# Feed-forward output projection computed by seven block products in place of eight, in three parts, with operands prepared in the feed-forward loop

## The chip, the cores and the metric

The kernel runs on one core of a Trainium2 chip. The metric is device time in microseconds (us) of one execution. A core has TensorE for matmuls (PE; its weight loads are listed apart, as PEld), VectorE (DVE), ScalarE (ACT), GpSimd (POOL) and SyncE (SP), which here only issues DMAs. ScalarE issues DMAs too (ACTq). Each engine works through its own list of instructions in order; semaphores order the engines against one another.

## The reference

One layer over 1024 tokens of width 1024, all in float32. Cut to what matters here:

```
x  = x + merged @ w_out                       # merged: four gated mixers
h2 = rmsnorm(x, g_ffn)
f_gate, f_up = split(h2 @ w_ffn_in, 2)        # w_ffn_in: 1024 x 5632
x  = x + (silu(f_gate) * f_up) @ w_ffn_out    # w_ffn_out: 2816 x 1024
h3 = rmsnorm(x, g_ple)
x  = x + sigmoid(h3 @ w_ple_gate) * (p @ w_ple_proj)
return rmsnorm(x, g_final)
```

## The kernel before

Activations lie transposed: a tile is 128 channels by 1024 tokens (512 KB). Each float32 matmul is made of three passes over reduced-precision parts: `split` writes a rounded part `hi` (copy on ScalarE) and the rest `lo` (subtraction on VectorE), and the product is hi·hi + hi·lo + lo·hi. Every matmul here is 128 x 128 by 128 x 512.

**Seven products.** The gate matmuls and the feed-forward input (`pair`, L537) compute two output tiles at once. Channels and tokens are cut in two blocks each, so that a 2 x 2 block product is done with seven block products in place of eight, at the price of sums: four over the weights (the generator `sums` in `pair`: L548, L551, L555, L557, on GpSimd), four over the activations (`operands`, L517, made once and kept in `OPS[p][i]`), and a few at the outputs. `product(p)` splits a weight sum (L563) into one of four buffers, and for four input pairs i runs three matmuls each (L568): 12 matmuls. Products 0, 2 and 4 accumulate in the same PSUM bank, with a ScalarE copy in between (L576, L583, L588). A call of `pair` is 84 matmuls.

**Feed-forward loop** (L695 to L715). 11 iterations over two hidden tiles each; an iteration is one `pair` for the gate and one for the up part, then silu and multiply. The two result tiles are stored to device memory by four DMAs of 256 KB on ScalarE's queue (L714).

**Feed-forward output** (L724 to L767). The 22 hidden tiles are the inner dimension and the 8 tiles of `x2` the outputs. `CHUNKS` cuts the inner dimension in two (14 and 8 hidden tiles), and `grp` the outputs in two groups of four. For each hidden tile the loop loads it (`load_parts`, L167), splits it, loads and splits its weights, and runs 4 x 3 x 2 matmuls (L740) into eight PSUM banks; the last part (L749 to L760) goes output tile by output tile. That is 22 x 8 x 3 x 2 = 1056 matmuls. `n3.add` (L767) then makes the parts and squares for the next norm: per tile two ScalarE and two VectorE operations of 1024 columns (L191, L192, L196, L200).

**Buffers.** `T` has 38 buffers of one tile; the feed-forward loop keeps 28 of them for `OPS` and one for the norm factor, and each `pair` takes two (`n15`, `n23`). `M` has 8, which before the loop pass to `x2` (L721). `W` has three for raw weights.

**Order.** A scheduler orders each engine's instructions ahead of time from the program's order and its own estimates: a weight split of the next pair can stand ahead of an output operation of this one. It also hands out buffers, in the order of the program.

Of the kernel before, what the change touches and what calls it, by code (L numbers as in the profile page):

```python
# [13 lines left out]
P = 128  # L14
# [10 lines left out]
CHUNKS = ((0, 14), (14, 22))  # L25
# [13 lines left out]
def mixers_kernel(ctx, tc, xT, pT, vec, mask, sgu_ln, sgu_wT, sgu_b, w_in, w_tok, w_gate, w_br, w_out,  # L39
# [26 lines left out]
    def M(name, w=S, dt=F32):  # L66
        return mp.tile([P, w], dt, tag="m", name=name, padded_shape=[P, S], bufs=8)
# [4 lines left out]
    def WS(name):  # L72
        return wp.tile([P, 512], F32, tag="sw", name=name, bufs=2)
# [278 lines left out]
    def qk(ct):  # L352
# [3 lines left out]
        for nm, i in (("q", 6 + ct), ("k", 8 + ct)):  # L356
            ps = proj_tile(i)
            t = T(f"{nm}{ct}")
            if nm == "q":
                nc.vector.scalar_tensor_tensor(t, ps, -(64.0 ** -0.5), rs, ALU.mult, ALU.mult)  # L360
                for h in range(2):
                    a, b = slice(h * 64, h * 64 + 64), slice(64 - h * 64, 128 - h * 64)
                    d = M(f"qs{ct}{h}", S, F32R)
                    nc.scalar.copy(d[a, :], t[a, :])
                    nc.vector.tensor_sub(d[b, :], t[a, :], d[a, :].bitcast(F32))
                    qs.append(d)
            else:
                nc.vector.tensor_mul(t, ps, rs)
                kl = M(f"kl{ct}", S, F32R)
                for h in range(2):  # L370
                    a, b = slice(h * 64, h * 64 + 64), slice(64 - h * 64, 128 - h * 64)
                    d = M(f"kd{ct}{h}", S, F32R)
# [60 lines left out]
    sgc = M("sgc", 6 * P).rearrange("p (g c) -> p g c", c=P)  # L433
# [83 lines left out]
    def operands(name, i, xa, xb, have=()):  # L517

        a1, a2, b1, b2 = xa[:, :512], xa[:, 512:], xb[:, :512], xb[:, 512:]
        t12, t34 = M(f"{name}t12i{i}"), M(f"{name}t34i{i}")  # L520
        t1, t2, t3, t4 = t12[:, :512], t12[:, 512:], t34[:, :512], t34[:, 512:]
        if 0 not in have:
            operand(name, 0, i, a1)
        nc.vector.tensor_sub(t1, a2, a1)
        operand(name, 1, i, t1)
        nc.vector.tensor_sub(t2, b2, t1)
        operand(name, 2, i, t2)
        if 3 not in have:
            operand(name, 3, i, b1)
        nc.vector.tensor_sub(t3, b2, a2)  # L530
        operand(name, 4, i, t3)
        if 5 not in have:
            operand(name, 5, i, b2)
        nc.vector.tensor_sub(t4, b1, t2)
        operand(name, 6, i, t4)

    def pair(name, wa, wb):  # L537

        ra = W(f"{name}ra")
        nc.sync.dma_start(ra, wa)  # L540
        rb = W(f"{name}rb")
        nc.sync.dma_start(rb, wb)
        a1, a2, b1, b2 = ra[:, :512], ra[:, 512:], rb[:, :512], rb[:, 512:]

        def sums():
            yield a1
            s1 = WS(f"{name}s1")
            nc.gpsimd.tensor_add(s1, b1, b2)  # L548
            yield s1
            s2 = WS(f"{name}s2")  # L550
            nc.gpsimd.tensor_sub(s2, s1, a1)  # L551
            yield s2
            yield a2
            s3 = WS(f"{name}s3")
# [6 lines left out]
        def product(p, src, ps, first):  # L561
            hi, lo = WP(f"{name}p{p}")
            split(hi, lo, src)  # L563
            for i in range(4):
                x = OPS[p][i]
                wh, wl = hi[:, i * P:(i + 1) * P], lo[:, i * P:(i + 1) * P]
                for n, (w, c) in enumerate(((wh, 0), (wh, 512), (wl, 0))):
                    nc.tensor.matmul(ps, w, x[:, c:c + 512], start=(first and i == 0 and n == 0),  # L568
                                     stop=(i == 3 and n == 2), skip_group_check=not first)
# [28 lines left out]
    def gate_operands(i):  # L598
# [6 lines left out]
        operands("g", i, xl[2 * i], xl[2 * i + 1], (0, 3, 5))  # L605
# [59 lines left out]
    for m0 in (0, 1, 2, 3, 4, 5, 6):  # L665
# [23 lines left out]
        if len(xgs) % 2 == 0:  # L689
            i = len(xgs) // 2 - 1  # L690
            operands("f", i, xgs[-2], xgs[-1])


    fd = []
    for j in range(0, NJ, 2):  # L695
# [28 lines left out]
    for ci, (k0, k1) in enumerate(CHUNKS):  # L724
        fs = {}
        for grp in range(2):
            last = ci == 1 and grp == 1
            if not last:
                ps = [[A(f"fo{ci}{grp}{mm}{h}") for h in range(2)] for mm in range(4)]
                for k in range(k0, k1):  # L730
                    if grp == 0:
                        fs[k] = load_parts(f"f{k}", fd[k])
                    if k % 2 == 0:
                        raw = W(f"fow{grp}{k}")
                        nc.sync.dma_start(raw, w_fo[:, (grp * NJ + k) * 512:(grp * NJ + k + 2) * 512])
                        w = w_parts(f"fow{grp}{k}", raw, S)
                    for mm in range(4):
                        for i, (n, p) in enumerate(((0, 0), (0, 1), (1, 0))):
                            for h in range(2):
                                nc.tensor.matmul(ps[mm][h], w[k % 2 * 4 + mm][n], fs[k].part(p, h * 512, h * 512 + 512),  # L740
                                                 start=(k == k0 and i == 0), stop=(k == k1 - 1 and i == 2))
            if ci == 1 and not last:
                for k in range(2):
                    raw = W(f"pp{k}r")
                    nc.sync.dma_start(raw, pT[k * P:(k + 1) * P, :])
                    pp.append(parts(f"pp{k}", raw))
            for mm in range(4):
                m = 4 * grp + mm
                if last:  # L749
                    pm = [A(f"fo{ci}{grp}{mm}{h}") for h in range(2)]  # L750
                    w = []
                    n = (k1 - k0) * P
                    for c in range(0, n, S):
                        e = min(c + S, n)
                        raw = W(f"fol{m}{c}", e - c)
                        nc.sync.dma_start(raw, w_fo[:, (NJ + k0) * 512 + mm * n + c:(NJ + k0) * 512 + mm * n + e])
                        w += w_parts(f"fol{m}{c}", raw, e - c)
                    for k in range(k0, k1):
                        for h in range(2):
                            mm_k(pm[h], w[k - k0], fs[k], k == k0, k == k1 - 1, ((h * 512, h * 512 + 512),), h * 512)  # L760
                else:
                    pm = ps[mm]
                for h in range(2):
                    t = x2[m][:, h * 512:h * 512 + 512]
                    nc.vector.tensor_add(t, pm[h], t)  # L765
                if ci == 1:
                    n3.add(m, x2[m])  # L767
# [101 lines left out]
def _layout(i):  # L869
# [15 lines left out]
    def taps(w):  # L885
# [22 lines left out]
    wo = a["w_ffn_out"][0].reshape(NJ, P, 2, 4, P)  # L908
    k1 = CHUNKS[1][0]
    out["w_fo"] = np.concatenate([t.reshape(P, -1) for t in (  # L910
        wo[:, :, 0].transpose(1, 0, 2, 3), wo[:k1, :, 1].transpose(1, 0, 2, 3), wo[k1:, :, 1].transpose(1, 2, 0, 3))], 1)
# [20 lines left out]
```

## Time and profile before

| | us |
|---|---|
| median of 3 runs | 1612.82 (1610.34 to 1613.44) |
| time of the profiled execution | 1612.55 |
| its span in the trace | 1610.8 |
| TensorE busy | 1588.8 (99%) |
| VectorE busy | 1031.6 (64%) |
| ScalarE busy | 640.0 (40%) |
| GpSimd busy | 215.1 (13%) |

The span runs from the first to the last instruction; 1.75 us of the execution's time lie around it. Busy shares are means over stages with different limits, so the rows below are read stage by stage. TensorE counts as busy while a matmul is under way; a matmul of 512 columns is listed with 389 ns, and the next may start before it ends.

### The profile page before, as it was taken

How to read it: one execution, taken by the hardware profiler on the slowest of the kernel's cores; microseconds unless marked ns; L12 is line 12 of the kernel's file. 1: busy time of each engine (PE TensorE's matmuls, PEld its weight loads, DVE VectorE, ACT ScalarE, POOL GpSimd, SP SyncE). 2: the span in 40 equal slices, each digit the busy share in tenths (PEclk: the TensorE clock that was granted, in tenths of full speed). 3: DMA queues.
4: the chain of work that ended last, by engine and by line, in shares of the span. 5: the costliest groups of instructions: out<-in, count | busy, mean ns of one | idle time of the engine just before them, and what ended most of it. 6: DMA issues, size and time to landing. Idle time of an engine off the chain costs nothing.

```text
span 1610.8 us, 19722 instructions
## 1 busy us (share of the span) xinstructions
PE 1588.8 (99%) x7626; PEld 1309.6 (81%) x7626; DVE 1031.6 (64%) x1506; ACT 640.0 (40%) x1068; POOL 215.1 (13%) x158
## 2 busy tenths in 40 slices
PE   9999999999999999999999999999999999999997
PEld 7976788778888888888888888888888888888886
DVE  6988785755567667686776666666666431354456
ACT  6335554233434334354553333433334411133334
POOL 0000000112222222200122322223220000000000
PEclk9999999999999999999999999999999999999998
DMA  6110233121212212213442222222225531211214
GB/s 223 53 40 14 70 129 108 66 79 47 92 53 72 66 52 73 66 59 135 140 176 79 85 79 87 94 82 79 81 89 172 207 92 53 68 41 46 66 47 141
DMA packets 46718, 140.93 MB, mean 87 GB/s; under 512 B 5280, under 2 KB 8608, under 8 KB 46624
## 3 DMA queue, kind: packets, MB, share of 16 engines
q1 hardware_dynamic: 39024, 125.98, 23.8%
q10 hardware_dynamic: 7600, 13.69, 2.3%
q8 instruction: 60, 0.98, 0.3%
q14 instruction: 34, 0.28, 0.1%
HBM read 115.53 MB, written 24.12 MB: 87 GB/s over the span
## 4 chain that ended last, share of the span: by engine, by line
PE 88%; DVE 8%; DMA 1%; ACT 1%; issue 0%; ACTq 0%; SPq 0%; DVEq 0%
PE fo L740 12%; PE pj L151 10%; PE wo L151 5%; PE br L151 5%; PE pg L151 5%; PE fo L151 3%; PE po L413 1%; PE sc L394 1%; PE pq L151 1%; PE ptp L407 1%; PE sc L393 1%; PE sp L317 1%; PE sp L315 1%; PE fu20u L568 1%; PE gt63u L568 1%; PE gt43u L568 1%
## 5 line engine op out<-in xcount | busy, mean ns | idle before, releaser
L330 DVE SCALAR_TENSOR_TENSOR cacc<-cy,vs,cacc 128x1023 f32<-128x1023 f32 (+29 forms) x60 | 75.7, 1263 | 0.5
L408 ACT COPY pt<-ptp 128x512 f32<-128x512 f32 (+3 forms) x48 | 21.8, 481 | 35.5 <-PE ptp L407 35.5
L814 DVE TENSOR_TENSOR pt<-pg,n3r 128x768 f32<-128x768 f32 (+1 forms) x16 | 11.0, 689 | 29.7 <-PE pg L151 29.7
L398 DVE CUSTOM_DVE_ANT_0 pr<-sc,maskt 128x128 f32<-128x128 f32 (+7 forms) x32 | 24.1, 753 | 9.1 <-PE sc L394 8.8
L151 PE MATMUL pj<-n1p,w1h 128*128 128x512 f32 x96 | 27.7, 408 | 1.4 <-ACT n1p L191 1.4
L765 DVE TENSOR_TENSOR x<-fo,x 128x512 f32<-128x512 f32 x32 | 20.9, 687 | 12.5 <-PE fo L151 11.3
L400 ACT ACTIVATE pr<-pr,nm 128x128 f32<-128x128 f32 (+7 forms) x32 | 24.9, 779 | 5.5 <-DVE nm L398 5.3
L438 POOL TENSOR_SCALAR_AFFINE_SELECT sgc<-sgc 128x512 f32<-128x512 f32 x1 | 1.3, 1322 | 168.8 <-DMA sgc<-in_sgu_wT 168.8
L151 PEld LDWEIGHTS pj<-n1p,w1h 128*128 128x128 f32 x96 | 18.7, 196 | 6.2 <-ACT n1p L191 2.2
L413 PE MATMUL po<-pt,vt 128*64 128x128 f32 x288 | 22.7, 279 | 0.2
L407 PE MATMUL ptp<-ident,pr 128*128 128x128 f32 x144 | 22.2, 276 | 0.0
L413 PEld LDWEIGHTS po<-pt,vt 128*64 128x64 f32 x288 | 16.9, 136 | 5.8 <-issue 2.8
L394 PE MATMUL sc<-kl,qs 64*128 64x512 f32 (+3 forms) x48 | 21.0, 438 | 0.0
L815 ACT ACTIVATE pt<-pt 128x768 f32<-128x768 f32 (+1 forms) x16 | 10.1, 630 | 26.3 <-DVE pt L814 26.3
L682 DVE TENSOR_TENSOR xr<-wo,xr 128x512 f32<-128x512 f32 x16 | 11.0, 688 | 14.8 <-PE wo L151 14.7
L407 PEld LDWEIGHTS ptp<-ident,pr 128*128 128x128 f32 x144 | 16.6, 140 | 3.1 <-ACT rb L418 1.0
L393 PE MATMUL sc<-kd,qs 128*128 128x512 f32 (+3 forms) x48 | 18.7, 390 | 0.1
L548 POOL TENSOR_TENSOR gt00s<-gt00rb 128x512 f32<-128x512 f32 x1 | 1.3, 1292 | 131.1 <-DMA gt00rb<-in_w_gate 131.1
L683 ACT ACTIVATE x1g<-xr,vs 128x512 f32<-128x512 f32 x16 | 11.6, 724 | 18.0 <-DVE xr L682 18.0
L394 PEld LDWEIGHTS sc<-kl,qs 64*128 64x128 f32 x48 | 8.8, 183 | 10.0 <-issue 8.6
L822 ACT ACTIVATE pt<-x 128x768 f32<-128x768 f32 (+1 forms) x13 | 8.4, 647 | 19.0 <-DVE x L818 19.0
L151 PE MATMUL pj<-n1p,w1l 128*128 128x512 f32 x48 | 15.3, 398 | 0.0
(4222 smaller groups left out, 5306.7 us busy)
## 6 DMA issues: line engine op xcount, KB each, us to landing
fow<-in_w_fo SPq DMA_DIRECT2D x18, 512.0 KB, 3.8
xg<-in_xT SPq DMA_DIRECT2D x8, 512.0 KB, 4.2
xr<-in_xT SPq DMA_DIRECT2D x8, 512.0 KB, 5.1
x1d<-xr SPq DMA_DIRECT2D x8, 512.0 KB, 2.9
x<-x1d SPq DMA_DIRECT2D x8, 512.0 KB, 5.8
x<-in_xT SPq DMA_DIRECT2D x7, 512.0 KB, 7.5
vpr<-in_w_tok SPq DMA_DIRECT2D x4, 512.0 KB, 4.8
spr<-in_w_tok SPq DMA_DIRECT2D x4, 512.0 KB, 3.6
```

The lines of the kernel that those rows point to most:

```text
L151: nc.tensor.matmul(ps[:, c - off:e - off], w[n], act.part(p, c, e), start=(first and i == 0), stop=(last and i == 2))
L330: nc.vector.scalar_tensor_tensor(acc[:, d:], y[:, :S - d], wj, acc[:, d:], ALU.mult, ALU.add)
L393: nc.tensor.matmul(sc[:, c:c + n], q, kd[h][:, c:c + n], start=True, stop=False)
L394: nc.tensor.matmul(sc[:, c:c + n], q[a, :], kl[a, c:c + n], start=False, stop=True)
L398: nc.vector.tensor_tensor_reduce(out=pr[:, :L], in0=sc[:, :L], in1=maskt[:, S - L:], scale=1.0, scalar=NEG, op0=ALU.add, op1=ALU.min, accu ...
L400: nc.scalar.activation(pr[:, :L], pr[:, :L], AF.Exp, bias=nm, scale=-1.0, accum_out=ls)
L407: nc.tensor.transpose(pa[:, j * P:(j + 1) * P], pr[:, c + j * P:c + (j + 1) * P], ident)
L408: nc.scalar.copy(pt[:, c:c + n], pa[:, :n])
L413: nc.tensor.matmul(po[h * 64:h * 64 + 64, :P], vtok[j // 4][:, hc:hc + 64], pts[h][:, j * P:(j + 1) * P], start=(j == 0), stop=(j == b))
L568: nc.tensor.matmul(ps, w, x[:, c:c + 512], start=(first and i == 0 and n == 0), stop=(i == 3 and n == 2), skip_group_check=not first)
L740: nc.tensor.matmul(ps[mm][h], w[k % 2 * 4 + mm][n], fs[k].part(p, h * 512, h * 512 + 512), start=(k == k0 and i == 0), stop=(k == k1 - 1 a ...
L765: nc.vector.tensor_add(t, pm[h], t)
```

## The change

The feed-forward output now goes through `pair`. The 22 hidden tiles are 11 input pairs, and `CHUNKS` cuts these into parts of 4, 4 and 3. In each part `pair` is called for four pairs of output tiles; with n input pairs a call has 7 x n x 3 matmuls. Its blocks are added to `x2`.

The seven activation operands of a hidden pair are made in the feed-forward loop (`operands("h", ...)`: four subtractions, seven splits), in buffers of `M`, and each is stored to device memory as it is made: seven DMAs of 512 KB per iteration on ScalarE's queue, in place of four of 256 KB. Each part of the output first loads its 28, 28 or 21 operand tiles into `T`, by SP. The splits of the hidden tiles in the output stage go away. The four weight sums of every `pair`, in the gates and the feed-forward input too, move from GpSimd to VectorE.

```diff
-CHUNKS = ((0, 14), (14, 22))
+CHUNKS = ((0, 4), (4, 8), (8, 11))
...
-    def operand(name, p, i, src):
-
-        t = T(f"{name}o{p}i{i}", F32R)
+    def operand(name, p, i, src, alloc=T):
+
+        t = alloc(f"{name}o{p}i{i}", F32R)
         split(t[:, :512], t[:, 512:], src)
-        OPS[p][i] = t
+        return t
+
+    def operands(name, i, a1, a2, b1, b2, have=(), alloc=T):
+
         t12, t34 = M(f"{name}t12i{i}"), M(f"{name}t34i{i}")
         t1, t2, t3, t4 = t12[:, :512], t12[:, 512:], t34[:, :512], t34[:, 512:]
+        for p, (src, sub) in enumerate(((a1, None), (t1, (a2, a1)), (t2, (b2, t1)), (b1, None), (t3, (b2, a2)),
+                                        (b2, None), (t4, (b1, t2)))):
+            if sub:
+                nc.vector.tensor_sub(src, *sub)
+            if p not in have:
+                yield p, operand(name, p, i, src, alloc)
...
         def sums():
             yield a1
-            s1 = WS(f"{name}s1")
-            nc.gpsimd.tensor_add(s1, b1, b2)
+            s1 = WS(f"{name}s1", w)
+            nc.vector.tensor_add(s1, b1, b2)
             yield s1
-            s2 = WS(f"{name}s2")
-            nc.gpsimd.tensor_sub(s2, s1, a1)
+            s2 = WS(f"{name}s2", w)
+            nc.vector.tensor_sub(s2, s1, a1)
...
-            nc.gpsimd.tensor_sub(s3, a1, b1)
+            nc.vector.tensor_sub(s3, a1, b1)
             yield s3
-            nc.gpsimd.tensor_sub(s2, a2, s2)
+            nc.vector.tensor_sub(s2, a2, s2)
...
-        for k in range(2):
-            d = tc.dram_tile([P, S], F32, name=f"fd{j + k}")
-            for h in range(2):
-                nc.scalar.dma_start(d[:, h * 512:h * 512 + 512], both[0][k, h])
-            fd.append(d)
+        f = both[0]
+        for p, t in operands("h", j // 2, f[0, 0], f[0, 1], f[1, 0], f[1, 1], (), M):
+            d = tc.dram_tile([P, S], F32, name=f"fd{p}{j}")
+            nc.scalar.dma_start(d, t.bitcast(F32))
+            fd[p].append(d)
...
-    for ci, (k0, k1) in enumerate(CHUNKS):
...
+    for ci, (i0, i1) in enumerate(CHUNKS):
+        n = i1 - i0
+        for p in range(7):
+            for i in range(n):
+                OPS[p][i] = T(f"ho{p}i{i0 + i}", F32R)
+                nc.sync.dma_start(OPS[p][i].bitcast(F32), fd[p][i0 + i])
+        if ci == 2:
+            for k in range(2):
+                raw = W(f"pp{k}r")
+                nc.sync.dma_start(raw, pT[k * P:(k + 1) * P, :])
+                pp.append(parts(f"pp{k}", raw))
+        c0, c1 = i0 * 2 * P, i1 * 2 * P
+        for m in range(0, KD, 2):
+            for k, h, ps, t in pair(f"fo{ci}{m}", w_fo[m, :, c0:c1], w_fo[m + 1, :, c0:c1], n):
+                x = x2[m + k][:, h * 512:h * 512 + 512]
+                nc.vector.tensor_add(x, x, t)
+                nc.vector.tensor_add(x, ps, x)
+            if ci == 2:
+                n3.add(m, x2[m])
+                n3.add(m + 1, x2[m + 1])
```

## Rows read from the trace of the kernel before

**Rows 1.** Page: busy time by engine; chain that ended last, by engine.

```profile
PE 1588.8 (99%) x7626; PEld 1309.6 (81%) x7626; DVE 1031.6 (64%) x1506; ACT 640.0 (40%) x1068; POOL 215.1 (13%) x158
...
PE 88%; DVE 8%; DMA 1%; ACT 1%; issue 0%; ACTq 0%; SPq 0%; DVEq 0%
```

**Rows 2.** Windows, columns as headed: gates; one loop iteration; output stage.

```profile
core 0: us, PE busy (x) PEld busy (x) DVE busy (x) ACT busy (x) POOL busy (x), PEclk, DMA share, GB/s
...
500.00:600.00 100.00, 100.00 (x443) 82.77 (x442) 69.47 (x102) 39.30 (x67) 23.57 (x16) 1.00 0.20 64
...
1035.10:1073.60 38.50, 38.38 (x170) 31.46 (x169) 25.42 (x34) 14.89 (x27) 10.75 (x8) 1.00 0.24 82
...
1232.70:1472.30 239.60, 239.60 (x1059) 198.40 (x1058) 94.75 (x116) 63.03 (x80) 0.00 (x0) 1.00 0.30 97
```

**Rows 3.** Timeline of TensorE (start us, us): where loop, output stage and tail begin.

```profile
806.52 0.62 PE L568 MATMUL fg0u<-fo0i,fg0p0h 128*128 128x512 f32 x2
...
1232.93 0.62 PE L740 MATMUL fo<-f0h,fow000h 128*128 128x512 f32 x2
...
1472.29 0.51 PE L151 MATMUL pq<-pp0h,wpp000h 128*128 128x512 f32 x2
```

**Rows 4.** Timeline of VectorE, beside GpSimd's work, in a dependent pair, and alone.

```profile
1040.91 1.67 DVE L709 TENSOR_TENSOR fg10n<-fg10n,fu10n 128x512 f32<-128x512 f32 x1
...
1043.70 0.68 DVE L704 TENSOR_TENSOR fu10n<-fu10n,n2r 128x512 f32<-128x512 f32 x1
1044.42 0.69 DVE L709 TENSOR_TENSOR fg10n<-fg10n,fu10n 128x512 f32<-128x512 f32 x1
...
1228.60 0.69 DVE L703 TENSOR_TENSOR fu20n<-fu20u,fu20n 128x512 f32<-128x512 f32 x1
1229.21 0.68 DVE L111 TENSOR_TENSOR fow00512l<-fow,fow00512h 128x512 fp32r<-128x512 f32 x1
1229.81 0.69 DVE L704 TENSOR_TENSOR fu20n<-fu20n,n2r 128x512 f32<-128x512 f32 x1
```

**Rows 5.** Timeline of GpSimd around the same time.

```profile
1040.35 1.68 POOL L557 TENSOR_TENSOR fg12s<-fg12ra,fg12s 128x512 f32<-128x512 f32 x1 [2.55 <-DVE fg12p2l L111]
```

**Rows 6.** Timeline of ScalarE: a store's issue, and the copy behind it.

```profile
1045.14 0.33 ACTq L714 DMA_DIRECT2D fd<-fg10n  x1
1045.51 0.59 ACT L576 COPY fg12n<-fg12u 128x512 f32<-128x512 f32 x1 [1.71 <-DVE fg10n L709]
```

**Rows 7.** Waits of TensorE's weight loads in the loop (us, times, longest).

```profile
PEld fg12u L568 <- ACT fg12n L576: 0.5, 1, 0.5
```

**Rows 8.** Windows of 5 us in which the DMA engines were nearly always busy.

```profile
810.00:815.00 5.00, 4.84 (x22) 3.72 (x21) 5.00 (x9) 4.10 (x8) 0.91 (x1) 1.00 0.93 347
815.00:820.00 5.00, 5.00 (x32) 4.39 (x31) 1.45 (x3) 2.58 (x5) 2.60 (x2) 1.00 0.77 285
820.00:825.00 5.00, 5.00 (x24) 4.09 (x23) 3.75 (x7) 1.69 (x4) 0.00 (x0) 1.00 0.95 372
```

**Rows 9.** DMA issues: count, KB each, median us from issue to landing.

```profile
fow<-in_w_fo SPq DMA_DIRECT2D x18, 512.0 KB, 3.8
...
fd<-fg12n ACTq DMA_DIRECT2D x4, 256.0 KB, 2.0
...
fd<-fg20n ACTq DMA_DIRECT2D x4, 256.0 KB, 3.0
```

**Rows 10.** Timeline of VectorE behind the last output tile.

```profile
1474.40 1.28 DVE L192 SCALAR_TENSOR_TENSOR n3l<-x,vs,n3h 128x1024 fp32r<-128x1024 f32 x1 [0.62 <-ACT n3h L191]
1475.60 1.22 DVE L200 TENSOR_TENSOR n3sq<-n3sq,n3sq 128x1024 f32<-128x1024 f32 x1
1476.74 0.68 DVE L111 TENSOR_TENSOR wpg01512l<-wpg01r,wpg01512h 128x512 fp32r<-128x512 f32 x1
```

**Rows 11.** Windows in which the granted clock fell.

```profile
1475.00:1480.00 5.00, 4.33 (x26) 3.82 (x25) 2.72 (x5) 2.37 (x4) 0.00 (x0) 0.81 0.08 26
1480.00:1485.00 5.00, 5.00 (x17) 4.32 (x16) 2.94 (x5) 0.41 (x1) 0.00 (x0) 0.50 0.00 0
```

More of the change, by code (lines that the diff above doesn't have):

```diff
@@ L70, in W, with WS @@
         return wp.tile([P, w], F32, tag="wr", name=name, padded_shape=[P, S], bufs=3)
-    def WS(name):
-        return wp.tile([P, 512], F32, tag="sw", name=name, bufs=2)
+    def WS(name, w=512):
+        return wp.tile([P, w], F32, tag="sw", name=name, padded_shape=[P, 512], bufs=2)
     def WP(name):
@@ L521, in operands @@
         t1, t2, t3, t4 = t12[:, :512], t12[:, 512:], t34[:, :512], t34[:, 512:]
[L522 to L534, printed above, removed]
@@ L535, in operands, with keep_operands @@
-        operand(name, 6, i, t4)
-    def pair(name, wa, wb):
-        ra = W(f"{name}ra")
+        for p, (src, sub) in enumerate(((a1, None), (t1, (a2, a1)), (t2, (b2, t1)), (b1, None), (t3, (b2, a2)),
[4 more added lines that the diff above has]
+                yield p, operand(name, p, i, src, alloc)
+    def keep_operands(name, i, xa, xb, have=()):
+        for p, t in operands(name, i, xa[:, :512], xa[:, 512:], xb[:, :512], xb[:, 512:], have):
+            OPS[p][i] = t
@@ L562, in product @@
             hi, lo = WP(f"{name}p{p}")
-            split(hi, lo, src)
-            for i in range(4):
+            split(hi[:, :w], lo[:, :w], src)
+            for i in range(n):
                 x = OPS[p][i]
                 wh, wl = hi[:, i * P:(i + 1) * P], lo[:, i * P:(i + 1) * P]
-                for n, (w, c) in enumerate(((wh, 0), (wh, 512), (wl, 0))):
-                    nc.tensor.matmul(ps, w, x[:, c:c + 512], start=(first and i == 0 and n == 0),
-                                     stop=(i == 3 and n == 2), skip_group_check=not first)
+                for j, (ww, c) in enumerate(((wh, 0), (wh, 512), (wl, 0))):
+                    nc.tensor.matmul(ps, ww, x[:, c:c + 512], start=(first and i == 0 and j == 0),
+                                     stop=(i == n - 1 and j == 2), skip_group_check=not first)
         src = sums()
@@ L604, in gate_operands @@
         OPS[0][i], OPS[3][i], OPS[5][i] = acts[2 * i].tiles[0], acts[2 * i + 1].tiles[0], acts[2 * i + 1].tiles[1]
-        operands("g", i, xl[2 * i], xl[2 * i + 1], (0, 3, 5))
+        keep_operands("g", i, xl[2 * i], xl[2 * i + 1], (0, 3, 5))
     ya = []
@@ L690, in mixers_kernel @@
             i = len(xgs) // 2 - 1
-            operands("f", i, xgs[-2], xgs[-1])
-    fd = []
+            keep_operands("f", i, xgs[-2], xgs[-1])
+    fd = [[] for _ in range(7)]
     for j in range(0, NJ, 2):
@@ L723, in mixers_kernel @@
     pp = []
-    for ci, (k0, k1) in enumerate(CHUNKS):
[L725 to L767, printed above, removed]
@@ new lines, in mixers_kernel @@
+    for ci, (i0, i1) in enumerate(CHUNKS):
+        n = i1 - i0
+        for p in range(7):
+            for i in range(n):
+                OPS[p][i] = T(f"ho{p}i{i0 + i}", F32R)
[14 more added lines that the diff above has]
+                n3.add(m + 1, x2[m + 1])
@@ L907, in _layout @@
     out["w_fi"] = halves(tiles(a["w_ffn_in"][0]))
[L908 to L911, printed above, removed]
+    wo = tiles(a["w_ffn_out"][0])
+    out["w_fo"] = np.concatenate([halves(wo[:, :, i * 2 * P:j * 2 * P]) for i, j in CHUNKS], 2)
     out["w_pg"] = tiles(a["w_ple_gate"][0])
```

21 lines of the change are left out of this document (11 added, 10 removed).

## The prediction

> **What bounds the kernel now.** The page comes first: TensorE is busy 99% of the span, and the chain that ended last runs 88% through it [rows 1]. So it is asked next whether a stage runs at TensorE's own rate or waits. The timeline answers for the output stage: its first matmul starts at 1232.93, the tail's first at 1472.29 [rows 3]. That is 239.36 us for 1056 matmuls, or 0.2267 us each, although each is listed with 0.39 us. The stage waits for nothing, VectorE is busy 94.75 of 239.6 us and the DMA engines 30% [rows 2]. Here fewer matmuls are time won, at 0.2267 us each, as long as nothing else becomes late.
>
> The loop starts at 806.52 and ends at 1232.93 [rows 3]: 426.4 us for 22 x 84 = 1848 matmuls, 418.9 us at that rate. 7.5 us are waits. An iteration takes 38.5 us; its 168 matmuls need 38.1, and 0.5 us is one wait of the weight load of product 2 for the copy of product 0's result [rows 7]. ScalarE's timeline shows why: the copy stands behind the issue of a store, which waited 1.71 us for the multiply it stores [rows 6], and that multiply took 1.67 us because GpSimd's sum ran beside it [rows 4, 5]. VectorE is busy 25.42 us of the iteration [rows 2], idle 13.1.
>
> **The change part by part.**
>
> *Matmuls.* 1056 become 4 x 7 x 3 x 11 = 924. 132 x 0.2267 = **29.9 us less**.
>
> *Weight sums to VectorE.* GpSimd took 1.68 us for one beside a VectorE operation [rows 5]. VectorE takes 0.69 for 512 columns, and the next independent one starts after 0.61, a dependent one after 0.72 [rows 4]. In the gates and the loop a pair gains four operations.
>
> *Operands in the loop.* Four subtractions, seven `lo` and seven `hi` per iteration. VectorE goes from 34 operations [rows 2] to 34 + 8 + 11 = 53: 53 x 0.61 = 32.3 us, or 38.2 if each depended on the one before, against TensorE's 38.1. ScalarE goes from 14.89 us to 14.89 + 7 x 0.59 plus three more issues of 0.33 [rows 6], about 20: no bound. Cost on the path: nothing below, if VectorE stays under 38 us; weight splits run up to four products ahead (four buffers, 10.9 us), which covers a burst. If that cover goes, a late split stops TensorE. Seven stores in place of four, each waiting for a `lo`: behind such an issue on ScalarE stands the copy that product 2 waits for, so the wait of 0.5 us can stay, go (5.5 us won over 11 iterations) or grow. I take 0: the multiply is no longer stretched by GpSimd, but there are more issues to wait behind. Bounds -5.5 and, from the rival below, +31.
>
> *Loading the operands.* This is what can eat the gain. A part's 28 tiles are 14.7 MB, and 28 of the 38 `T` buffers are the ones the pair before still reads. A buffer comes free when its three matmuls are done, every 3 x 0.2267 = 0.68 us, and its successor is needed one pair (84 matmuls, 19.04 us) later, again every 0.68 us. The DMA engines are slower. Nearly saturated they moved 335 GB/s on the mean of three windows and 372 in the best [rows 8]: 1.56 and 1.41 us per tile. I take the middle, 1.48. Landing adds 3.8 - 1.4 = 2.4 us [rows 9].
>
> Into part 1: of 38 buffers 28 hold `OPS`, one the norm factor, four the results in flight, so five tiles are loaded early. 23 remain, from 18.4 us before the loop's end to 18.4 us after it, when the last one is needed: 36.8 us. In that time also come two weight tiles and the last iteration's seven stores: 32 tiles x 1.48 + 2.4 = 49.8, **13.0 us late**. Best rate 10.7, mean rate 15.5; if the stores took their turn behind the loads, 25 tiles, 2.6. I count the stores: the last iteration's stores of 256 KB already landed in 3.0 us in place of 2.0 when loads ran beside them [rows 9]. The Trainium skill (DMA: Bandwidth & Descriptors, on queues, rings and completion order) says that each DMA engine takes turns between the queues that have work, packet by packet; the slower stores agree, and by that rule the stores delay the loads, 13.0 rather than 2.6.
>
> Into part 2: six spare buffers, 22 tiles and four of weights in 36.8 us: 26 x 1.48 + 2.4 = 40.9, **4.1 us late** (2.3 to 6.2). Into part 3: 15 tiles and three of weights need 29.0 us, and the last is due 32 us after the first release: nothing.
>
> `x2` can only load once `M` is free of the last iteration's operands, some 5 us past the loop's end, behind the tiles above. Its first use is three products into the first pair; VectorE would wait there, and behind it the next pair's splits. The wait above gives TensorE the same delay, so I count 0 (bound: eight loads ahead of the last operands, below).
>
> *Part 3 and the tail.* A pair is 63 matmuls, 14.3 us. VectorE has 11 operations of 384 columns (0.46 each by columns), 8 of 512 and `n3.add` twice, 1.20 + 1.14 from start to start [rows 10]: 5.0 + 4.9 + 4.7 = 14.6, so 0.3 us over per pair, 1.2 in all. Before, only tile 7's norm work stood behind the last matmul; now tile 6 is complete 2 us before the end, and part of its 2.3 us stands ahead of tile 7's: some 1 us more. **2.2 us**, bounds 0 and 6.
>
> *Elsewhere.* The gates' two extra microseconds of VectorE per pair lie under TensorE, where VectorE was busy 69.47 of 100 us [rows 2]. More DMA traffic costs no matmul: at 372 GB/s TensorE was busy all 5 us, with 24 matmuls under way, as many as elsewhere [rows 8].
>
> Sum: -29.9 + 13.0 + 4.1 + 2.2 = -10.6. From the profiled execution's 1612.55 that gives 1602.0; the median of the three runs is 0.27 above that execution, which changes nothing that can be measured: this kernel's runs can tell a change of about 0.2%, 3.2 us.
>
> **The rivals.**
>
> *Loads hidden.* If the stores fall behind the loads, or more buffers are spare than I count, part 1 is at most 2.6 us late. Against it stand the count of buffers and the slowed stores. With 2.6 and 2.3 at the transitions, 2.2 in the tail and the 5.5 us of loop waits gone: 1612.55 - 29.9 + 7.1 - 5.5 = 1584.
>
> *VectorE becomes the bound of the loop (slower).* The 13.1 us in which it idles per iteration are waits for casts and matmuls [rows 2], and the operands add a chain (subtract, cast on ScalarE, subtract) with more of them. It needs 32.3 us; the change loses as a whole when an iteration passes 38.5 + 10.6/11 = 39.5, that is when more than 7.2 of the 13.1 us remain idle. With nine it is 41.3, 2.8 more, 31 in 11 iterations: 1633; with eight, 1622. For it: VectorE takes its list in order, and an output operation that waits for TensorE holds all behind it. Against: it has 19 more operations to put in those gaps, and lead of several products.
>
> *Transitions worse (slower or equal).* With `x2`'s eight tiles ahead of the last operands and the mean rate: 40 x 1.56 + 2.4 - 36.8 = 28.0, and 6.2 into part 2: -29.9 + 34.2 + 2.2, 1619.
>
> *The clock.* In the tail, where TensorE was busy only 4.33 of 5 us, the granted clock fell to 0.81 and then 0.50, that is 1.2 GHz, for 5 us [rows 11]. Waits of a microsecond between products at a transition may do the same; while loads set the pace half speed costs nothing, as a product then takes 5.4 us against 4 x 1.48 = 5.9 for its tiles, and when that is over 5 us at half speed lose 2.5 us at each of two transitions: 1607. The Trainium skill (TensorE: Matmul & The Clock Gate, on oscillation) describes a matmul kernel whose clock fell at every wait for a DMA; the loop's waits of 0.5 us did no such thing here, with the clock at 1.00 [rows 2].
>
> **How the numbers follow.** My forecast, with part of the gain lost at the transitions (1594 to 1609, the clock's case within it): 0.45. Loads hidden, below 1594: 0.17. Within 3.2 us of no change, where a worse transition or one more microsecond per iteration leads: 0.12. VectorE as bound: 0.16. Transitions worse: 0.10. Faster 0.62, same 0.12, slower 0.26. The range for 8 in 10 leaves out the end of each side: 1585 to 1625. The likeliest case alone: 1594 to 1609.
>
> **What would show it.** The output stage's 924 matmuls at 0.2267 us, 209.5 us without waits; TensorE's waits there named by DMA of `ho` tiles, some 13 us before the first pair ends and 4 at the second part, with the DMA engines above 300 GB/s; none at the third. In the loop 53 VectorE operations per iteration, none stretched past 0.75 us, and iterations of 38 to 39 us. An iteration of 40 us or more with TensorE waiting for `lo` parts would make the prediction wrong on the slow side; an output stage below 215 us, on the fast side.

## The result, and the profile after

The changed kernel takes 1692.93 us (median of 4 runs, 1688.58 to 1693.8), the kernel before beside it 1611.58: a ratio of 1.0502 [1.0475, 1.0529]. The forecast was 1602.0 with a range to 1625. The change costs 81 us where 10.6 were to be won; between the two profiled executions it is 80.5.

Page of the changed kernel, busy time by engine and the chain that ended last [rows 1]:

```profile
PE 1583.7 (94%) x7494; PEld 1298.3 (77%) x7494; DVE 1202.3 (71%) x1909; ACT 702.0 (42%) x1211; POOL 1.1 (0%) x6
...
PE 85%; DMA 6%; DVE 6%; ACT 2%; issue 1%; ACTq 0%; SPq 0%; DVEq 0%
```

The 132 matmuls are gone (7626 to 7494), but TensorE's share fell from 99% to 94% of a longer span. DMA is now 6% of the chain. The timeline of TensorE says in which stage [rows 3]:

```profile
806.00 0.62 PE L564 MATMUL fg0u<-fo0i,fg0p0h 128*128 128x512 f32 x2
...
1276.62 0.62 PE L564 MATMUL fo00u<-ho0i,fo00p0h 128*128 128x512 f32 x2
...
1556.19 0.50 PE L151 MATMUL pq<-pp0h,wpp000h 128*128 128x512 f32 x2
```

The loop takes 470.6 us (426.4 before), the output stage 279.6 (239.4 before), the tail 135.1 up to the span's end (138.5 before). So +44.2 and +40.2, and both have to be explained. Windows of the gates, one iteration, the output stage, the first pairs of parts 1 and 2, the gap ahead of part 3, and part 3's first pair [rows 2] (a pair is counted from its first matmul to the next pair's first; in names parts count from 0, so `fo12` is the pair of output tiles 2 and 3 in part 2):

```profile
core 0: us, PE busy (x) PEld busy (x) DVE busy (x) ACT busy (x) POOL busy (x), PEclk, DMA share, GB/s
500.00:600.00 100.00, 100.00 (x443) 82.84 (x442) 74.39 (x118) 39.84 (x68) 0.00 (x0) 1.00 0.21 64
1060.20:1103.10 42.90, 40.22 (x170) 32.48 (x169) 33.21 (x54) 18.54 (x33) 0.00 (x0) 0.96 0.38 135
1276.60:1556.20 279.60, 220.97 (x926) 178.56 (x925) 159.53 (x253) 89.73 (x153) 0.00 (x0) 0.88 0.53 198
1276.60:1332.00 55.40, 24.38 (x85) 18.21 (x84) 19.69 (x33) 9.68 (x17) 0.00 (x0) 0.66 0.85 327
1389.10:1421.60 32.50, 21.57 (x85) 16.72 (x85) 10.71 (x17) 6.29 (x11) 0.00 (x0) 0.84 0.82 325
1478.70:1495.50 16.80, 0.23 (x2) 0.05 (x1) 3.02 (x4) 0.51 (x1) 0.00 (x0) 0.57 0.94 372
1495.50:1512.60 17.10, 17.10 (x63) 13.90 (x64) 13.09 (x25) 7.05 (x14) 0.00 (x0) 0.83 0.16 47
```

In the gates nothing changed but the engine of the sums. In the iteration VectorE has 54 operations in 33.21 us, as forecast, and is idle for 9.7; yet the iteration takes 42.9 us. In the output stage 924 matmuls at 0.2267 us are 209.5 us, so 70 us are waits: 36.4 in the first pair of part 1 (55.4 for 19.0), 13.5 in that of part 2, 16.8 ahead of part 3, and 2.9 in part 3's first pair, in which TensorE is busy throughout but at a granted clock of 0.83 (17.2 for 14.3). That makes 69.6.

**The loop.** Waits of TensorE's weight loads [rows 7], then ScalarE's timeline [rows 6]:

```profile
PEld fg12u L564 <- ACT fg12p4h L110: 3.1, 1, 3.1
```

```profile
1066.42 0.62 ACT L110 CAST ho2i<-ht12i 128x512 fp32r<-128x512 f32 x1
...
1070.24 0.62 ACT L110 CAST ho6i<-ht34i 128x512 fp32r<-128x512 f32 x1
1072.21 0.33 ACTq L710 DMA_DIRECT2D fd<-ho4i  x1
1072.81 0.33 ACTq L710 DMA_DIRECT2D fd<-ho5i  x1
1073.41 1.11 ACTq L710 DMA_DIRECT2D fd<-ho6i  x1
1074.57 0.59 ACT L575 COPY fg12n<-fg12q 128x512 f32<-128x512 f32 x1 [3.71 <-PE fg12c L564]
1075.05 0.59 ACT L579 COPY fg12n<-fg12u 128x512 f32<-128x512 f32 x1
1075.55 0.63 ACT L702 ACTIVATE fg12n<-fg12n 128x512 f32<-128x512 f32 x1
1076.08 0.60 ACT L110 CAST fg12p4h<-fg12s 128x512 fp32r<-128x512 f32 x1
```

TensorE waits 3.1 us for the cast of product 4's weights. Its sum was ready at 1070.97 (VectorE L551, from 1070.28, 0.69 us). The cast ran at 1076.08, because ScalarE's list has ahead of it the issues of three stores, which wait for the `lo` parts, and then two copies and a silu. The copy's bracket names a matmul of product 3, but the copy starts 0.05 us after the last issue ended (1073.41 + 1.11). All ten iterations after the first show such a wait, of 3.1 to 4.0 us. ScalarE is busy 18.54 of 42.9 us: it is late, not full.

The wait is not the whole price. The granted clock is 0.92 to 0.96 in each of these ten iterations, and TensorE is busy 39.7 to 41.0 us in them. Where the same list ran at 1.00 (the run with the load order, last section) it was busy 38.62. Over ten iterations that is some 15 us, an estimate from these rows; the other 29 of the 44.2 us are the waits, less the old 0.5 us per iteration.

**Part 1.** Timeline of SyncE's queue:

```profile
1259.10 0.33 SPq L538 DMA_DIRECT2D fo00rb<-in_w_fo  x1
1259.52 1.92 SPq L725 DMA_DIRECT2D ho0i<-fd  x4
...
1265.27 5.44 SPq L725 DMA_DIRECT2D ho2i<-fd  x4
1272.96 0.32 SPq L725 DMA_DIRECT2D ho3i<-fd  x1
1283.43 14.98 SPq L717 DMA_DIRECT2D x<-x1d  x8
1298.46 1.37 SPq L725 DMA_DIRECT2D ho3i<-fd  x3
1299.93 2.31 SPq L725 DMA_DIRECT2D ho4i<-fd  x4
1302.98 4.15 SPq L725 DMA_DIRECT2D ho5i<-fd  x4
1308.10 4.15 SPq L725 DMA_DIRECT2D ho6i<-fd  x4
```

The first operand load comes right behind a weight load, 17.1 us before the loop's end; no spare buffer was filled ahead. The eight `x2` loads stand in the middle of the operands. They wait for buffers of `M` until 1283.43, so that SyncE issues nothing for 10 us, and then take 15 us themselves. Fifteen operand tiles stand behind them. TensorE waits 20.0 us for `ho3i` and 10.6 in product 6, which stands ahead of products 2, 5 and 4 in its list and whose tiles are loaded last.

**Part 2 and part 3.** SyncE's queue again, then the matmul that waits in part 2, and the cast that waits in part 3:

```profile
1371.62 0.33 SPq L538 DMA_DIRECT2D fo10rb<-in_w_fo  x1
1372.00 2.66 SPq L725 DMA_DIRECT2D ho0i<-fd  x4
...
1398.41 4.15 SPq L725 DMA_DIRECT2D ho6i<-fd  x4
...
1484.97 0.33 SPq L536 DMA_DIRECT2D fo20ra<-in_w_fo  x1
```

```profile
1408.72 1.19 PE L564 MATMUL fo10e<-ho6i,fo10p6h 128*128 128x512 f32 x2 [10.63 <-DMA ho6i<-fd]
```

```profile
1494.89 0.51 ACT L110 CAST fo20p0h<-fo20ra 128x384 fp32r<-128x384 f32 x1 [18.92 <-DMA fo20ra<-in_w_fo]
```

Part 2's loads begin at 1372.00, two microseconds into the pair before (its first matmul is at 1370.1), right behind a weight load that got its buffer at 1371.62. The six spare buffers were not filled ahead. From 1377 to 1410 the DMA engines are full:

```profile
1377.00:1410.00 33.00, 22.07 (x94) 17.39 (x93) 13.25 (x21) 6.91 (x12) 0.00 (x0) 0.89 1.02 408
```

Product 6 runs ahead of product 2 on TensorE, but its tiles are loaded last. Ahead of part 3 it is the weights that are late: their load stands behind 21 operand loads.

### The profile page after: what moved, and what is told of

Read it like the earlier page. It is cut to its first block, busy times and chain, and to the rows that moved or that the text cites. A ratio compares the mean times of both kernels' runs of the same rounds, so it can differ in the third digit from the quotient of the medians.

```text
span 1691.3 us, 19947 instructions
## 1 busy us (share of the span) xinstructions
PE 1583.7 (94%) x7494; PEld 1298.3 (77%) x7494; DVE 1202.3 (71%) x1909; ACT 702.0 (42%) x1211; POOL 1.1 (0%) x6
## 4 chain that ended last, share of the span: by engine, by line
PE 85%; DMA 6%; DVE 6%; ACT 2%; issue 1%; ACTq 0%; SPq 0%; DVEq 0%
PE pj L151 10%; PE wo L151 5%; PE br L151 5%; PE pg L151 5%; DMA ho4i<-fd 2%; PE po L413 1%; DMA ho6i<-fd 1%; PE sc L394 1%; PE pq L151 1%; PE ptp L407 1%; PE sc L393 1%; DMA fd<-ho6i 1%; PE fg8u L564 1%; DMA ho2i<-fd 1%; PE fg20u L564 1%
## 5 line engine op out<-in xcount | busy, mean ns | idle before, releaser
L564 PE MATMUL fo00c<-ho3i,fo00p3h 128*128 128x512 f32 x8 | 3.9, 589 | 19.7 <-DMA ho3i<-fd 19.7
L678 DVE TENSOR_TENSOR xr<-wo,xr 128x512 f32<-128x512 f32 x16 | 11.0, 688 | 15.6 <-PE wo L151 15.6
L787 ACT ACTIVATE pt<-pt 128x768 f32<-128x768 f32 (+1 forms) x16 | 10.1, 630 | 26.3 <-DVE pt L786 26.3
L564 PEld LDWEIGHTS fo00c<-ho3i,fo00p3h 128*128 128x128 f32 x8 | 1.9, 279 | 20.8 <-DMA ho3i<-fd 20.7
```

Of the source, the lines that this page charges most:

```text
L564: nc.tensor.matmul(ps, ww, x[:, c:c + 512], start=(first and i == 0 and j == 0), stop=(i == n - 1 and j == 2), skip_group_check=not first)
L678: nc.vector.tensor_add(t, ps, t)
```

## The experiments

Each kernel's ratio is to the kernel before on the same chip.

**The sums alone** (kernel before, the four weight sums on VectorE).

```diff
-            nc.gpsimd.tensor_add(s1, b1, b2)
+            nc.vector.tensor_add(s1, b1, b2)
...
```

> The kernel before, with only the four weight sums of every pair moved from GpSimd to VectorE. Theory A (the loop's 44 us come from the operands and stores that stand in ScalarE's list ahead of the next weight cast; the sums are harmless): the loop keeps 426 us or loses the 0.5 us wait per iteration, so 1606 to 1613 us, the same within 0.4%. Theory B (VectorE's list is what makes weights late; eight more operations per iteration lengthen it): the loop grows by 10 us or more, 1622 or above.

Measured: 1605.85 us, ratio 0.9971 [0.9958, 0.9985]. One iteration:

```profile
1037.40:1075.50 38.10, 38.10 (x169) 31.54 (x169) 26.63 (x43) 14.88 (x26) 0.00 (x0) 1.00 0.26 83
```

The wait of 0.5 us for the copy [rows 7] is gone, and an iteration takes its matmuls' 38.1 us: theory A. This part of the change is a small gain, and this kernel is the fastest complete one of the study.

**The changed kernel with the sums back on GpSimd** (the four lines reversed).

> The changed kernel with the four weight sums back on GpSimd, all else as changed. Theory A: product 4 of the gate pair still waits for its cast behind the operand casts and store issues, the loop stays above 455 us (changed: 470.6) and the time above 1675. Theory B: with eight operations fewer on VectorE the loop falls to 430 to 440 us and the time to 1655 to 1662.

Measured: 1679.18, ratio 1.042 [1.0391, 1.0448]; iterations of 40.5 to 43.3, loop 453.6, output stage 281.4. Theory A's 455 is missed by 1.4 us, theory B's 430 to 440 by 13.6. The loop is 17.0 us better, but not cured, and most of the 17 is not work taken off VectorE: nine of its eleven iterations ran at a granted clock of 1.00, against one in the changed kernel. In the iterations from 1000 us on TensorE now waits up to 2.8 us for the third copy in place of the cast:

```profile
PEld fg16u L564 <- ACT fg16n L579: 2.8, 1, 2.8
```

It is still something in ScalarE's list, though VectorE has less to do: the waits are 2.3 to 3.4 us in place of 3.1 to 4.0. That leaves ScalarE's own list as the suspect.

**Operand stores issued by SyncE.**

```diff
-            nc.scalar.dma_start(d, t.bitcast(F32))
+            nc.sync.dma_start(d, t.bitcast(F32))
```

> The changed kernel with the seven operand stores per iteration issued by SyncE in place of ScalarE. Theory A, part issues: six issues that wait for lo parts leave ScalarE's list, the cast for product 4 comes 2 to 3 us earlier, iterations fall from 43 to 39 to 41 us, the time to 1650 to 1672. If the casts alone make it late (or theory B holds), iterations stay at 42 us or more and the time above 1680.

Measured: 1648.36, ratio 1.0229; loop 422.0 us. One iteration:

```profile
1036.30:1074.40 38.10, 38.10 (x169) 31.52 (x168) 33.15 (x54) 18.88 (x33) 0.00 (x0) 1.00 0.42 152
```

VectorE's and ScalarE's work is the same as in the changed kernel's iteration (33.15 and 18.88 us), the bytes are the same, and the iteration is 38.1 with the clock at 1.00, better than the 39 to 41 expected: all of the loop's 44 us, waits and clock, came from the store issues in ScalarE's list. (With them gone the copies also stand earlier in that list; the two weren't told apart.) The output stage stays at 281.5 us, with 59.9 in part 1's first pair.

**No operand loads** (stores by SyncE; the output stage loads no operands and multiplies by those that the loop holds, so its output is another).

```diff
-        for p in range(7):
-            for i in range(n):
-                OPS[p][i] = T(f"ho{p}i{i0 + i}", F32R)
-                nc.sync.dma_start(OPS[p][i].bitcast(F32), fd[p][i0 + i])
```

> Stores on SyncE, and no operand is loaded in the output stage: its products read the operands that the feed-forward loop left in its buffers, so the output is another. What is left is the output stage's own matmuls, weights, sums and the norm. If all its waits come from the loads, the stage takes 210 to 216 us (924 matmuls at 0.2267 are 209.5) against 281.5 with loads, and the time is 1577 to 1584 us. If VectorE, the weights or x2 hold it up too, the stage takes 225 us or more.

Measured: 1587.5, ratio 0.985 [0.9821, 0.9878]. The output stage:

```profile
1228.60:1446.70 218.10, 212.39 (x926) 174.43 (x925) 159.89 (x253) 90.05 (x153) 0.00 (x0) 0.98 0.27 91
```

218.1 us, 2 more than the 210 to 216 expected; the time, 1587.5, misses its 1577 to 1584 too. 8 us are lost in the second pair, where TensorE waits 6.0 for a cast whose weights `fo02rb` stand in SyncE's list behind the eight `x2` loads. Against 281.5 with the loads, exchanging the operands costs 63 us, and but for those 8 the stage needs its matmuls' time.

**`x2` loaded pair by pair, behind part 1's operands** (stores by ScalarE, as in the change).

```diff
-    for m in range(KD):
-        x2.append(M(f"x2{m}"))
-        nc.sync.dma_start(x2[m], x1d[m])
...
+            if ci == 0:
+                for k in range(2):
+                    x2.append(M(f"x2{m + k}"))
+                    nc.sync.dma_start(x2[m + k], x1d[m + k])
```

> The changed kernel with each pair of x2 tiles loaded in front of the pair of the first part that needs it, behind that part's operand loads in the program. Theory C (SyncE's list: the eight x2 loads wait for buffers of M ahead of the last 15 operand tiles): the first pair of part 1 falls from 55.4 to 30 to 36 us, as in part 2 (32.5), and the time to 1668 to 1676. Rival D (the transition is bound by what the DMA engines move): the pair stays above 48 us, as the same bytes have to come.

Measured: 1679.23, ratio 1.042. The first pair takes 42.8 us in place of 55.4, between theory C's 36 and rival D's 48; the second takes 20.3, the others are unchanged (32.9 in part 2). So `x2` ahead of the operands cost 12.6, and 24 us remain in part 1. There the DMA engines were full from 1255 to 1304 (share 1.01, 392 GB/s), from the first operand load, which again stood behind a weight load, to the last tile. So D's cause has a part in these 24.

**Operand tiles loaded in the order in which TensorE uses them.**

```diff
-        for p in range(7):
+        for p in (0, 1, 3, 6, 2, 4, 5):
```

> The changed kernel with each part's operand tiles loaded in the order of products 0, 1, 3, 6, 2, 4, 5, in which TensorE's list of the changed kernel first touches them, in place of 0 to 6. Theory E (part 2's first pair takes 32.5 us because TensorE's list has a piece of product 6 in fourth place, and its tile lands last, with three products queued behind it): that pair falls to 20 to 24 us and part 1's by about 10; 1668 to 1682 us. Rival D (the loading itself sets the length): part 2's first pair stays above 29 us.

Measured: 1690.51, ratio 1.0489; part 2's first pair 31.9 us against 32.5, and part 1's 55.2 against 55.4. Theory E is missed, and the rival's condition (above 29 us) is met. ScalarE's timeline in that pair:

```profile
1408.47 0.62 ACT L110 CAST fo12p0h<-fo12ra 128x512 fp32r<-128x512 f32 x1 [14.77 <-DMA fo12ra<-in_w_fo]
1408.99 0.58 ACT L579 COPY fo10n<-fo10u 128x512 f32<-128x512 f32 x1
```

The wait for `ho6i` is gone, and TensorE waits 5.0 us at product 5 and then 4.8 for this copy. The copy stands behind the next pair's first weight cast, whose load stands behind the operand loads. One order was mended, and the next one took its place; whether the loading itself would have held the pair as long, this run does not say.

**Weights first** (stores by SyncE, `x2` pair by pair; `then` are the part's operand loads, given to its first pair and so behind its weights; `pp` is loaded behind part 3's first pair).

```diff
-    def pair(name, wa, wb, n=4):
+    def pair(name, wa, wb, n=4, then=None):
...
         nc.sync.dma_start(rb, wb)
+        if then:
+            then()
```

> Stores on SyncE, x2 loaded pair by pair, and in each part the weights of the first pair loaded ahead of the operand tiles; the two tiles of p behind the last part's first pair. Theory F (at part 3 TensorE waits 16 us for weights that stand behind 21 operand loads in SyncE's list): fo16 to fo20 falls from 34.6 to 19 to 22 us; part 1's first pair, now with stores and loads in one list, 38 to 50. Time 1612 to 1628, against 1648 with the stores on SyncE alone. If part 3's operands are as late as its weights, the wait stays above 10 us and the time above 1628.

Measured: 1634.14, ratio 1.0139; stage 267.6. The gap ahead of part 3 is gone (`fo16` to `fo20` 19.1 us in place of 34.6), but part 3's first pair now takes 21.9 and waits 5.6 for operands, and the time misses 1612 to 1628. Part 2's first pair is 32.6, not moved. Part 1's is 52.7: less than with the stores on SyncE alone (59.9), but 10 us more than with `x2` pair by pair and the stores on ScalarE (42.8).

**A small first part** (as weights first, but stores by GpSimd; four parts, of at most 21 tiles, so that more `T` buffers are spare).

```diff
-CHUNKS = ((0, 4), (4, 8), (8, 11))
+CHUNKS = ((0, 2), (2, 5), (5, 8), (8, 11))
```

> Stores issued by GpSimd, which has nothing else to do there, x2 and weights as in the run weights_first, and four parts of 2, 3, 3 and 3 hidden pairs, so that the first part needs 14 tiles, and 18 to 20 buffers are spare for the second. By the account of bytes (1.28 us a tile, as measured in part 2) no transition is late by more than 3 us: output stage 212 to 222 us, loop 420 to 424, time 1578 to 1592, faster than the kernel before. If GpSimd's stores hold up VectorE, iterations are above 38.5 us; if the lists rather than the bytes decide, transitions still cost over 10 us each and the time is above 1600.

Measured: 1654.35, ratio 1.0264; first pairs 26.7, 30.7, 27.6 and 26.3 us, where matmuls need 9.5 and 14.3: the expected 1578 to 1592 is missed by far, and transitions cost over 10 us each. Iterations of 39.4 us in place of 38.1 also say that GpSimd is a worse place for the stores than SyncE. SyncE's queue ahead of part 2:

```profile
1287.72 0.33 SPq L536 DMA_DIRECT2D fo10ra<-in_w_fo  x1
1294.27 0.33 SPq L538 DMA_DIRECT2D fo10rb<-in_w_fo  x1
1294.65 2.25 SPq L726 DMA_DIRECT2D ho0i<-fd  x3
```

Spare buffers did nothing: the pair before begins at 1291.9, and the first load comes 2.7 us later all the same, behind weights that wait for a buffer.

**Loads named early** (as before, with up to 12 tiles of each next part named ahead of the pair before it).

```diff
+            if m == KD - 2 and ci < len(CHUNKS) - 1:
+                fetch(ci + 1, (0, 1, 3, 2))
             for k, h, ps, t in pair(f"fo{ci}{m}", w_fo[m, :, c0:c1], w_fo[m + 1, :, c0:c1], n,
```

> The run small_first_part, in which a part's loads began only some 2 us into the pair before it, with the first 12 tiles of each next part (four in front of part 1) named in the program ahead of the pair before it, so that they get spare buffers before that pair's results do; the rest after its weights. Theory G (loads are late because buffers are handed out in the program's order, not because none is free, and because SyncE's list holds them behind weights): parts 2, 3 and 4 lose at most 3 us each at their start (30.7, 27.6 and 26.3 us for first pairs of 14.3 before), part 1 keeps its wait for x2; output stage 225 to 235 us against 273.4, time 1604 to 1616. If the bytes decide, the first pairs stay above 24 us and the time above 1640.

Measured: 1623.8, ratio 1.0079; first pairs 12.3, 15.2, 15.6 and 16.7 us, stage 244.0 in place of 273.4. In parts 2 to 4 the first pairs lose the 3 us at most that theory G gave; the total is 8 us above its range, as part 1's four pairs take 59.0 us for 38.1 and part 4's second 20.8 for 14.3. Only the loads' place and order in the program changed, and 29 us went. Order within a part alone had won 0.6 us (in the parts of 4, 4 and 3); so it is most likely the late start, and that came from the program, which orders buffers and SyncE's list.

**Stores on two queues** (loads early; the first ten iterations' stores by SyncE, the last one's and `x2` by GpSimd).

> The run early_loads with the stores of the first ten iterations issued by SyncE, only the last iteration's by GpSimd, and x2 loaded by GpSimd behind them. Theories A, C and G together: loop 420 to 424 us as with the stores on SyncE, no list holds operand loads behind x2, output stage 212 to 222 us; time 1580 to 1594, faster than the kernel before and than the sums alone (1606). If part 1 still waits for x2 or stores, 1595 to 1605.

Measured: 1611.67, ratio 1.0011 [0.9997, 1.0024], as the kernel before, and above both ranges expected. The loop is 424.3 us, the stage 242.1. Part 1 has only two input pairs and loses 18.5 us: 56.6 for 38.1 of matmuls. The largest waits there are 5.4 us for a `lo`, behind output adds left over from the pairs before (VectorE is busy 16.76 of that pair's 17.7 us), and 3.1 for a cast. In the other parts pairs take 14.3 to 19.5 us for 14.3 of matmuls.

**Three parts with all of this** (4, 4 and 3; one product's four tiles named early, as many as there are spare buffers).

> The changed kernel with its parts kept at 4, 4 and 3 input pairs, and all that the runs so far have shown: operand stores off ScalarE's queue (SyncE for the first ten iterations, GpSimd for the last), x2 pair by pair on GpSimd's queue, the weights of a part's first pair ahead of its operand loads, and one product's operands (four tiles, as many as there are spare buffers) named ahead of the preceding pair. Theory G (loads start late because buffers are handed out in program order, and then the part is loaded at 1.28 us per tile): 24 tiles then remain from 2.7 us into the preceding pair, 24 x 1.28 = 30.7, done at 33.4 us, while the last product begins at 35.4: first pairs of parts 2 and 3 of 19 to 22 and 14.3 to 17 us where they took 32.6 and 21.9 (without the early tiles), that of part 1 25 to 32 where it took 52.7; an output stage of 218 to 232 us, a loop of 422 to 425, and in all 1589 to 1604 us, faster than before. Rival (a part of 28 tiles in 38 buffers cannot be exchanged under one pair, however early the loads are named; only smaller parts can): first pairs as in the run with the weights first, a stage above 255 us, and 1620 or more.

Measured: 1623.02, ratio 1.0066 [1.005, 1.0083]. First pairs 48.6, 28.9 and 15.3: part 3's as the theory has it, those of parts 1 and 2 neither's; the stage is 256.2, against 267.6 with the weights first. (Part 3's second pair takes 20.1 us, with VectorE busy 18.53: `pp`'s splits and the norm's work meet there since `pp` was moved.) TensorE's largest waits are 17.3 and 7.0 us, both for a copy on ScalarE:

```profile
1271.27 0.62 ACT L110 CAST fo02p0h<-fo02ra 128x512 fp32r<-128x512 f32 x1 [27.76 <-DMA fo02ra<-in_w_fo]
1271.80 0.58 ACT L581 COPY fo00n<-fo00u 128x512 f32<-128x512 f32 x1
```

**Weights apart** (as the last; weights of all pairs but a part's first issued by GpSimd).

```diff
-        nc.sync.dma_start(ra, wa)
+        (nc.gpsimd if name[:2] == "fo" and not then else nc.sync).dma_start(ra, wa)
```

> As the run with the parts of 4, 4 and 3 and one product named early, and the weights of all pairs of the output stage but a part's first are issued by GpSimd in place of SyncE, so that they do not stand behind the 24 operand loads in SyncE's list. In that run the first pair of part 1 took 48.6 us with one wait of 17.3 for ScalarE's copy fo00n, and that of part 2 28.9 with one of 7.0 for fo10n; each copy stood in ScalarE's list behind the cast of the next pair's first weights, which waited 27.8 and 11.5 us for their DMA. Theory: it is this order that costs the time, not the loading of the operands: the two waits go, first pairs of 29 to 34 and 20 to 23 us, a stage of 228 to 238 us in place of 256, 1596 to 1606 us in all, faster than before. Rival (the operands themselves arrive too late, and the copy only hides it): TensorE waits as long for DMA of operand tiles, first pairs above 44 and 27 us, 1618 to 1625.

Measured: 1627.8, ratio 1.0085 [1.0064, 1.0107]. The two waits for copies went, and a wait as long came one pair later: by first matmuls the first pairs take 17.9 and 16.3 us, the second ones 48.4 and 30.0. Both pairs of part 1 together take 66.3 us (67.7 before this edit), those of part 2 46.3 (47.9), for 38.1 of matmuls. The theory's time is missed, and the rival's (1618 to 1625) by 3 us. TensorE's and GpSimd's timelines, then windows of 10 us:

```profile
1272.09 1.22 PE L566 MATMUL fo02q<-ho1i,fo02p1h 128*128 128x512 f32 x2 [16.91 <-ACT fo02p1h L110]
...
1273.54 1.05 PE L566 MATMUL fo00u<-ho2i,fo00p2h 128*128 128x512 f32 x2
```

```profile
1253.14 0.53 POOL L538 DMA_DIRECT2D fo02rb<-in_w_fo  x1 [1.96 <-issue]
```

```profile
1225.00:1235.00 10.00, 10.00 (x46) 8.26 (x45) 9.40 (x16) 3.38 (x7) 0.54 (x1) 1.00 1.02 387
...
1245.00:1255.00 10.00, 7.67 (x24) 4.69 (x22) 1.04 (x2) 0.62 (x1) 2.11 (x4) 0.83 1.02 419
1255.00:1265.00 10.00, 0.17 (x1) 0.00 (x0) 0.00 (x0) 0.00 (x0) 2.12 (x4) 0.77 1.03 417
1265.00:1275.00 10.00, 2.91 (x7) 2.29 (x8) 4.28 (x7) 1.59 (x3) 0.53 (x1) 0.50 1.03 410
```

The 17.9 us are not a pair done: TensorE's list now has the second pair's product 0 and the first matmuls of its product 1 ahead of the first pair's products 2, 5 and 4, which ran from 1273.54 on. Product 1 waited for a cast whose weights `fo02rb` stood in GpSimd's list behind four `x2` loads; VectorE waited 19.0 us for them, as they landed 17.5 us after their issue. Meanwhile the tiles of the first pair's product 2 had been there since 1241.2. So an order still held TensorE up.

The bytes held it up too. From 1225 to 1275 the DMA engines are full, at 410 GB/s on the mean: 20.5 MB, 39 tiles, at 1.28 us each, operands, the last iteration's stores, `x2` and weights. Part 1's last operand tile landed at 1269.6, 18 us after 1252.0, when the first pair was due to end. So the theory that only order was left falls, but how the 28 us lost in part 1's two pairs divide between order and bytes isn't shown.

## Why the prediction was wrong

*Matmuls: right.* 29.9 us less; without loads the stage took 218.1 us, 8 of them waits.

*Weight sums on VectorE: right, and undervalued.* 54 operations and 33.2 us per iteration (53 and 32.3 forecast), none of it on the path once the stores are off ScalarE's list (iterations of 38.1). Alone they win 4.7 us (1605.85 against 1610.55). The forecast's reading of the old wait was off by a step: the store ahead of the copy waited for the multiply at 1044.42, which took 0.69 us, and the stretched one of 1.67 stood earlier in VectorE's list [rows 4]. That it made the later one late fits; that the wait goes with the sums is what was shown.

*Operands in the loop, cost 0, bounds -5.5 and +31: the step that failed first.* It cost 44.2, some 15 of them by a lower granted clock, which the forecast did not expect in the loop. The text named the right list (stores on ScalarE's queue, with a copy behind them) and took its growth for 0. It looked at one instruction behind the issues, the copy for product 2. Behind seven issues, each bound to a `lo` from VectorE, also stood the next weight cast. That weight splits run up to four products ahead was taken from the number of buffers; in the changed list the cast stood behind the stores, whatever buffer was free. The rival *VectorE as bound* gave the length of the iteration well (41.3 with nine microseconds idle; 42.9 measured with 9.7) and the cause wrongly: with the same VectorE work and the stores on SyncE the iteration is 38.1.

*Loading the operands, 13.0 + 4.1 + 0: mis-sized, by its start and its order.* Measured 36.4, 13.5 and 19.7. In part 1 the failed sentence is that `x2` loads "behind the tiles above": it stood ahead of fifteen of them and held SyncE's list for 25 us. The rival *transitions worse* had that mechanism, at 28.0; without it 24 us remain. In parts 1 and 2 the spare buffers, counted as five and six tiles loaded early, were not used: the loads stood behind weights in SyncE's list. Naming loads ahead of the pair before won 29 us over four parts, and 11.4 of the stage (267.6 to 256.2, with `x2` and the last stores on GpSimd's queue as well) with the parts as in the change. In part 3 the weights were overlooked: its 21 tiles did not delay the operands' first use, but the weights behind them by 16.8.

The rate per tile was too slow in the forecast: 1.28 us were measured, not 1.48, and with it the forecast's own sums give 6.6 us for part 1 and nothing for part 2. So the sums failed not by the rate but by what they took as loaded early and as loaded last. Bytes counted all the same: the engines were full through part 2's load. The 1.48 came from windows in which the engines were 77 to 95% busy [rows 8]; full, they moved 387 to 419 GB/s in the windows shown above. The kernel before had a full window too, at its start, which the forecast did not look at:

```profile
10.00:15.00 5.00, 5.00 (x23) 4.08 (x22) 4.30 (x6) 5.00 (x8) 0.00 (x0) 1.00 1.04 407
```

The Trainium skill (Perfetto Trace Analysis, Roofline) puts the ceiling of one active core's 16 DMA engines at about 435 GB/s; the rows here lie below it, the highest at 419.

*The clock: half right.* At the transitions it fell to half as expected, 1.2 GHz (a mean of 0.57 over the gap ahead of part 3). That half speed costs nothing while loads set the pace held in the gaps, but part 3's first pair lost 2.9 us after its gap, with TensorE busy throughout. In the loop, where the forecast saw no fall, it was 0.92 to 0.96 in the iterations with waits of 3.1 to 4.0 us.

*Part 3 and the tail, +2.2:* part 3's later pairs took 14.4 to 14.7 us; the tail, at 135.1 against 138.5, shows no cost.

*What stays open.* Whether a version of the block products beats the sums alone wasn't settled: the best one equals the kernel before. It would need fewer bytes at the first transition, or the second pair's weights ahead of `x2` and of the last operands; neither was tried, nor were the last iteration's stores left on ScalarE with the others on SyncE.

## What to carry to other kernels

Ask for every DMA issue that is added to a computing engine what it waits for and which later instruction of that engine TensorE needs next: issues that waited for another engine's results cost this kernel 44 us while both engines had idle time. A load is only as early as its place in the queue's list and in the program that hands out buffers, so write down that list at each change of stage, with weights and other small loads in it, before dividing bytes by a rate. When one order is mended, look for the next; when the wait only moves, look whether the DMA engines are full, and with what.

## What the runs showed of the hardware

In the windows shown, of 10 us and more, full DMA engines moved 387 to 419 GB/s, and 410 on the mean of 50 us in the run with the weights apart: 1.28 us for a tile of 512 KB. The forecast's best window had 372 [rows 8].

Two busy queues shared the engines about evenly. In the run with the weights apart, from 1246 to 1258 us, SyncE's and GpSimd's lists each issued a tile every 2.5 us, twice 1.28, and in that stage a tile took 17 to 20 us from issue to landing, in place of 3.8 [rows 9].

Waits of the same length in the loop had two prices. In the run with the load order, whose loop is that of the changed kernel, the waits are 3.1 us too, but in two of the ten iterations after the first the granted clock stayed at 1.00 and an iteration took 41.3 us, in place of 42.9 at 0.96 (with `x2` later it was five of ten):

```profile
1059.60:1100.90 41.30, 38.62 (x170) 31.35 (x169) 33.12 (x54) 18.53 (x34) 0.00 (x0) 1.00 0.40 140
```

Stores issued by GpSimd in place of SyncE lengthened the iteration from 38.1 to 39.4 us. In the run with the small first part TensorE waits 1.2 to 2.4 us in each iteration after the first for the copy ahead of product 2 of the up pair (`fu12n`, L574); why that copy is late was not looked into.
